# The last weight chunks of a block product rounded and split in another order, the fourth in a tile of its own, and a half-bank copy moved

## The chip, the cores and the metric

The kernel runs on one core of one Trainium2 chip. The time is device microseconds of one launch; lower is better. TensorE is called PE here, VectorE DVE, ScalarE ACT, GpSimd POOL; SP issues transfers.

## The reference

One decoder block on a sequence of 512 positions with model width 1024, in float32: a gated sub-layer with two mixers, then RMSNorm with modulation, a SwiGLU feed-forward of width 2816 with a gated residual, and a final RMSNorm. What matters here is the end:

```python
f_g, f_u = jnp.split(h2 @ w_ffn_in, 2, axis=-1)
x = x + gate2 * ((jax.nn.silu(f_g) * f_u) @ w_ffn_out)
...
return rms_norm(x, final_norm_g)
```

## The kernel before

**Precision.** Every float32 operand of a matmul is kept as a rounded half "hi" and a remainder "lo", and one product is three matmuls (`mm3`, L53 to L55: hi x hi, hi x lo, lo x hi). For a weight chunk (256 rows x 512 columns, 512 KB) ACT makes hi (the *rounding*, L114, "ACTIVATE hi<-raw") and DVE makes lo = raw - hi (the *split*, L118).

**Weights** come as a stream. `add_w` appends a chunk to it, with `where` as the home of its two halves; without one they rotate through three pairs of tiles named hi and lo. `issue` loads a raw chunk through SP's queue into one of three raw tiles, so the load of a chunk waits for the split of the chunk three before it. `get(i, ahead)` sees to it that the stream is rounded and split up to `ahead` chunks past i. Within an engine everything runs in the order of the program text (`manual_schedule`); waits between engines are put in by the framework from the tiles that are read and written.

**The end.** The down projection (gate product times w_ffn_out) is computed as seven block products after a Strassen-like scheme. Each accumulator Z[n] is two PSUM banks, one for each tile of 128 positions; Z[0] and Z[1] belong to positions 0 to 255 (tiles 0, 1), Z[2] and Z[3] to 256 to 511 (tiles 2, 3); even n holds columns 0 to 511, odd n columns 512 to 1023. `zprod` runs a block product chunk by chunk, with a list of tasks for the other engines at each chunk; `plain` adds the two rows of weight tiles that the scheme leaves over (its chunks are W_FO, here called the W_FO chunks). The last block product, key (1, 1), has five chunks (`zs`, called chunk 0 to 4, or the first to the fifth) and adds into Z[1] alone. It is written out as three passes: e = 0 (tile 0, 512 columns wide), then e = 1 in two passes of 256 columns. The second of these writes another bank, `last`, into which ACT copies the right half of Z[1][1] beforehand (the *half-bank copy*, L1867 before).

**Residuals.** `res(n, tk)` is a multiply by the gate (DVE, L1258), an add into x (DVE, L1259) and a square with a sum (ACT, L1263). `row_rstd` sums a row's parts (DVE, L1269, the *row sum*) and raises to -1/2 on POOL (L1270); `finish` scales the row (DVE, L1781) and stores it; `scale_g` (L1769) multiplies by the norm's gain ahead of `finish_last`.

**Order before the change.** Chunk 0 is rounded with the last `get` in `zprod`, chunk 1 after residual (0, 1), chunk 2 right behind it; chunk 3 after residual (3, 2), when the loop begins; chunk 4 in the loop, after the residuals (3, 3), (2, 2) and (2, 3). Homes: chunk 0 S2 tiles 6 and 7, chunk 1 S2 tiles 2 and 3, chunk 2 E1, chunks 3 and 4 the rotating pairs.

Of the kernel before, what the change touches and what calls it, by code (L numbers as in the profile page):

```python
# [10 lines left out]
F32R = mybir.dt.float32r  # L11
I32 = mybir.dt.int32
AF = mybir.ActivationFunctionType
# [15 lines left out]
def block_kernel(ctx: ExitStack, tc: tile.TileContext, x, positions, w_ada, b_ada, w_in,  # L29
# [3 lines left out]
    T, V, A, P, SY = nc.tensor, nc.vector, nc.scalar, nc.gpsimd, nc.sync  # L33
    ctx.enter_context(tc.manual_schedule())
    base = ctx.enter_context(tc.tile_pool(name="base", bufs=1))
# [6 lines left out]
    def bank(k, name="bank"):  # L42
        return psum.tile([128, 512], F32, name=name, tag=f"b{k}", bufs=1)

    def f(ap):
        return ap.bitcast(F32)
# [4 lines left out]
    def mm3(o, wl, rl, start, stop, **kw):  # L51
        (wh, wlo), (rh, rlo) = wl, rl
        T.matmul(o, wh, rh, start=start, stop=False, **kw)  # L53
        T.matmul(o, wh, rlo, start=False, stop=False, **kw)  # L54
        T.matmul(o, wlo, rh, start=False, stop=stop, **kw)  # L55


    stream, wseq, chunk = [], [], {}
# [5 lines left out]
    def add_w(src, kts, c0, n, lo=None, where=None):  # L64
        stream.append(dict(kind="w", src=src, kts=kts, c0=c0, n=n, lo=lo or V, where=where))
        wseq.append(len(stream) - 1)
        return len(stream) - 1
# [29 lines left out]
    def prep(i):  # L97
        e = stream[i]
        if e["kind"] == "m":
            e["fn"](e["raw"])  # L100
            return
        m = len(e["kts"]) * e["n"]
        if e["where"] is None:
            hi = base.tile([128, 1024], F32R, name="hi", tag="hi", bufs=3)
            lo = base.tile([128, 1024], F32R, name="lo", tag="lo", bufs=3)
        elif isinstance(e["where"], tuple):
            hi, lo = (s2home(k, name="wx") for k in e["where"])
        else:
            t = ffn[0].tile([128, 2, 1024], F32R, name="wx", tag=e["where"], bufs=1)
            hi, lo = t[:, 0], t[:, 1]  # L110
        if i == W1[0]:
            V.tensor_copy(hi[:, :m], e["raw"][:, :m])
        else:
            A.activation(hi[:, :m], e["raw"][:, :m], AF.Copy)  # L114
        if e["lo"] == "later":
            e["do"] = lambda: V.tensor_sub(lo[:, :m], e["raw"][:, :m], f(hi[:, :m]))
        else:
            e["lo"].tensor_sub(lo[:, :m], e["raw"][:, :m], f(hi[:, :m]))  # L118
        chunk[i] = (e["view"](hi), e["view"](lo))

    def ensure(upto):
        upto = min(upto, len(stream) - 1, st["limit"] - 1)
        while True:
            for i in range(st["prep"], min(st["prep"] + 16, len(stream), st["limit"])):
                if "raw" in stream[i]:
                    continue
                if room(i):
                    issue(i)
                elif stream[i]["kind"] == "w" or not stream[i]["mid"]:
                    break  # L130
            if st["prep"] > upto:
                break
            prep(st["prep"])
            st["prep"] += 1
# [13 lines left out]
    def get(i, ahead=2):  # L148
        k = wseq.index(i)
        ensure(wseq[min(k + ahead, len(wseq) - 1)])  # L150
        return chunk[i]
# [37 lines left out]
    ffn = []  # L189
# [113 lines left out]
    W_Z = {}  # L303

    def add_z(key, where=(None,) * 5):
        W_Z[key] = []
        for c in range(5):
            if key in wsum:
                src, k0, c0 = wsum[key], 2 * c, 0
            else:  # L310
                src, k0, c0 = w_ffn_out, KZ[key[0]][2 * c], key[1] * 512
            W_Z[key].append(add_w(src, [k0, k0 + 1], c0, 512, where=where[c]))
# [3 lines left out]
    W_FO = [add_w(w_ffn_out, KC, 0, 512, where="E7")]  # L316
    add_z(4)
    W_FO.append(add_w(w_ffn_out, KC, 512, 512, where="E0"))
    add_z((1, 1), ((6, 7), (2, 3), "E1", None, None))

    def wsum_steps():

# [26 lines left out]
    for i in range(4):  # L349
        t = base.tile([128, D], F32, name=f"x{i}", tag=f"X{i}", bufs=1)  # L350
# [31 lines left out]
    ch = chain.append  # L382
# [175 lines left out]
    for kt in range(8):  # L558
        hi, lo = chunk[W1[kt]]
# [338 lines left out]
    for h in range(2):  # L898
        pb = [bank(b, "pav") for b in range(4)]
        for i in W_AV[h]:  # L900
# [10 lines left out]
            hi, lo = get(i)  # L911
# [353 lines left out]
    def resid(p, c0, n, slot, tk, gate):  # L1265
        resid_b(resid_a(p, c0, n, tk, gate), c0, n, slot, tk)

    def row_rstd(tk):
        V.tensor_reduce(r2[:, tk:tk + 1], ss2[:, tk], op=OP.add, axis=AX.X)  # L1269
        P.tensor_tensor(r2[:, tk:tk + 1], r2[:, tk:tk + 1], mhalf[:, :1], op=OP.pow)  # L1270
# [179 lines left out]
    for half in range(2):  # L1450
        for h in range(2):
            po = O[2 * half + h]

            def res(e):
                resid(po[e], 512 * h, 512, h, 2 * half + e, gate_b[1])

            for n_, i in enumerate(W_O[2 * h:2 * h + 2]):
                hi, lo = chunk[i]
# [177 lines left out]
    for half in range(2):  # L1636
        o = slice(half * 256, (half + 1) * 256)
        for w in range(2):
            for ci, i in enumerate(W_F[w]):
                hi, lo = chunk[i]  # L1640
# [126 lines left out]
    def scale_g(c0, n, tk):  # L1767
        cs_ = slice(c0, c0 + n)
        V.tensor_mul(x_out()[tk][:, cs_], xt[tk][:, cs_], fng[0][:, cs_])  # L1769
# [10 lines left out]
    def finish(tk):  # L1780
        V.scalar_tensor_tensor(x_out()[tk], xt[tk], r2[:, tk:tk + 1], fng[0], op0=OP.mult, op1=OP.mult)  # L1781
        SY.dma_start(out[tk * 128:(tk + 1) * 128, :], xo[tk])


    Z, ZB = {}, ((4, 7), (0, 1), (2, 3), (5, 6))

    def zprod(k, ka, kw, start, tasks):
        if start:
            Z[k] = [bank(ZB[k][e], "pfo") for e in range(2)]
        for c, i in enumerate(W_Z[kw]):  # L1790
            wh, wl = get(i)
            for fn in tasks[c]:
                fn()
            ah, al = za[ka, c // 2]
            for e in range(2):
                o = slice(e * 128, (e + 1) * 128)
                for j in range(2):
                    k_ = 2 * (c % 2) + j
                    mm3(Z[k][e], (ah[:, k_, o], al[:, k_, o]), (wh[:, j], wl[:, j]),
                        start and c + j == 0, c + j == 5, skip_group_check=True)  # L1800
# [12 lines left out]
    def z_add(dst, src, op):  # L1813
        for e in range(2):
            op(Z[dst][e], Z[dst][e], Z["s", src][e])

    def hi_(key, c):
        return lambda: a_hi(key, c)

    def lo_(key, c):  # L1820
        return lambda: a_lo(key, c)
# [30 lines left out]
    def plain(o, tk, n, c=slice(0, 512)):  # L1852
        hi, lo = get(W_FO[n])
        opt_a_mm(o, tk, hi[:, :, c], lo[:, :, c], KC, gT, 22, False)
# [4 lines left out]
    def res(n, tk):  # L1859
        return lambda: resid(Z[n][tk % 2], 512 * (n % 2), 512, n % 2, tk, gate_b[2])  # L1860

    zprod(2, "A22", 4, False, [[hi_("S4", 2), lo_("S4", 2)], [lambda: z_add(3, 2, V.tensor_sub)],
                               [lambda: z_add(1, 3, V.tensor_add)], [res(0, 0)], [res(0, 1)]])
    zs = W_Z[1, 1]
    ch = [get(zs[0])]
    last = bank(7, "pfo")
    A.activation(last[:, :256], Z[1][1][:, 256:], AF.Copy)  # L1867
    for tk in range(2):
        plain(Z[3][tk], 2 + tk, 1)
    scale_g(0, 512, 1)  # L1870
    ch.append(get(zs[1], 1))
    res(3, 2)()
    for tk in range(2):
        plain(Z[2][tk], 2 + tk, 0)
    ch.append(get(zs[2], 1))
    tasks = {(0, 0): [res(3, 3)], (0, 1): [res(2, 2), lambda: row_rstd(2)], (0, 2): [res(2, 3), lambda: row_rstd(3)],
             (0, 3): [lambda: finish(2)], (0, 4): [lambda: finish(3)]}
    for e, z in ((0, None), (1, 0), (1, 1)):
        c = slice(0, 512) if z is None else slice(256 * z, 256 * z + 256)
        o = Z[1][0] if z is None else (Z[1][1], last)[z][:, :256]  # L1880
        t = slice(e * 128, (e + 1) * 128)
        n = c.stop - c.start
        for k, i in enumerate(zs):
            if k == len(ch):
                ch.append(get(i, 1))
            hi, lo = ch[k]
            for fn in tasks.pop((e, k), []):
                fn()
            ah, al = za["S4", k // 2]
            for j in range(2):  # L1890
                k_ = 2 * (k % 2) + j
                mm3(o, (ah[:, k_, t], al[:, k_, t]), (hi[:, j, c], lo[:, j, c]), False, False, skip_group_check=True)
        plain(o, e, 1, c)
        if z is None:
            resid(o, 512, n, 1, e, gate_b[2])
            row_rstd(e)
            finish(e)
        elif z == 0:
            resid(o, 512, n, 1, e, gate_b[2])
            scale_g(512, n, e)  # L1900
        else:
            resid(o, 768, n, 2, e, gate_b[2])
            row_rstd(e)
            scale_g(768, n, e)
            finish_last(e)
# [49 lines left out]
```

## Time and profile before

| | us |
|---|---|
| median of 3 runs | 813.89 (813.73 to 814.85) |
| the profiled execution's own time | 813.89 |
| span of the profile, first to last instruction | 812.1 |
| PE busy | 792.3 (98%) |
| weight load busy | 705.6 (87%) |
| DVE busy | 689.2 (85%) |
| ACT busy | 422.8 (52%) |
| chain that ended last, share of PE | 89% |

The profile shows one execution. Times in it count from the first instruction; a row of the timeline gives start and duration in us, engine, line, operation, output and inputs, and in brackets how long the engine sat idle before it and what released it. A busy PE is matmuls in a pipeline, whose ends are modelled, so that rows overlap: the spacing of starts tells the rate. The stretch that the change touches runs from about 765 us to the end.

### The profile page before, as it was taken

The numbers are of one execution on the slowest core, as the hardware profiler recorded it, in microseconds if no ns is written. First come the engines' busy times: TensorE is split into PE (matmuls) and PEld (weight loads), VectorE is DVE, ScalarE is ACT, GpSimd is POOL, SyncE is SP. The second block draws the span as 40 slices with busy tenths as digits, with TensorE's granted clock in tenths as the row PEclk, the third lists the DMA queues.
The fourth block names the chain that finished last, engine by engine and source line by source line (L and its number), as shares of the span: only waits on it lengthen the run. The fifth ranks groups of instructions, "written<-read, shape, count | busy, mean of one in ns | idle before, by whom it ended". The sixth has DMA issues, their size and how long they took to land.

```text
span 812.1 us, 12511 instructions
## 1 busy us (share of the span) xinstructions
PE 792.3 (98%) x4746; PEld 705.6 (87%) x4746; DVE 689.2 (85%) x1153; ACT 422.8 (52%) x727; POOL 137.2 (17%) x141
## 2 busy tenths in 40 slices
PE   7999999999999999999999999999999999999966
PEld 7889888888888888898888899999999999888855
DVE  7989788898899877787698779898999998987764
ACT  6674445323322255665536586566655556756441
POOL 3060031362344411000000011201111110000000
PEclk9999999999999999999999999999999999999998
DMA  9964352434336741147630528989997975556522
GB/s 317 336 174 120 104 182 79 115 92 130 110 123 207 222 142 52 52 157 233 196 117 25 183 78 200 265 230 253 273 274 199 281 193 173 178 185 199 191 77 105
DMA packets 104844, 138.44 MB, mean 170 GB/s; under 512 B 6560, under 2 KB 72736, under 8 KB 104624
## 3 DMA queue, kind: packets, MB, share of 16 engines
q1 hardware_dynamic: 92608, 106.15, 41.5%
q0 software_dynamic: 9584, 27.07, 14.2%
q10 hardware_dynamic: 2592, 4.42, 1.5%
q8 instruction: 37, 0.61, 0.3%
q14 instruction: 23, 0.19, 0.1%
HBM read 135.26 MB, written 23.07 MB: 195 GB/s over the span
## 4 chain that ended last, share of the span: by engine, by line
PE 89%; DVE 5%; ACT 3%; issue 2%; DMA 1%; POOL 0%; POOLq 0%; SPq 0%; ACTq 0%; DVEq 0%
PE pb L55 9%; PE pb L54 9%; PE pb L53 9%; PE R L54 8%; PE R L55 8%; PE R L53 8%; PE pfo L54 3%; PE pfo L55 3%; PE pfo L53 3%; PE pgb L53 2%; PE pgb L54 2%; PE pgb L55 2%; PE pav L54 2%; PE pav L53 2%; PE pav L55 2%
## 5 line engine op out<-in xcount | busy, mean ns | idle before, releaser
L114 ACT ACTIVATE hi<-raw 128x1024 fp32r<-128x1024 f32 (+2 forms) x98 | 101.5, 1039 | 87.3 <-DMA raw<-in_w_proj_a_dram 22.8
L54 PE MATMUL pb<-s,hi 128*128 128x512 f32 (+1 forms) x320 | 122.8, 384 | 0.0
L53 PE MATMUL pb<-s,hi 128*128 128x512 f32 (+1 forms) x256 | 98.8, 386 | 0.0
L55 PE MATMUL pb<-s,lo 128*128 128x512 f32 (+1 forms) x256 | 97.9, 383 | 0.0
L118 DVE TENSOR_TENSOR lo<-raw,hi 128x1024 fp32r<-128x1024 f32 (+2 forms) x62 | 75.1, 1214 | 26.0 <-ACT hi L114 25.7
L118 POOL TENSOR_TENSOR lo<-raw,hi 128x1024 fp32r<-128x1024 f32 x29 | 73.0, 2518 | 131.2 <-ACT hi L114 130.2
L54 PEld LDWEIGHTS pb<-s,hi 128*128 128x128 f32 x320 | 60.1, 188 | 10.9
L55 PEld LDWEIGHTS pb<-s,lo 128*128 128x128 f32 x256 | 48.1, 188 | 8.8
L53 PEld LDWEIGHTS pb<-s,hi 128*128 128x128 f32 x256 | 48.1, 188 | 8.4
L205 DVE SCALAR_TENSOR_TENSOR acc<-mraw,cols,acc 128x512 f32<-128x512 f32 x49 | 43.1, 879 | 3.7 <-DMA mraw<-in_w_ada_dram 2.9
L1270 POOL TENSOR_TENSOR sm<-sm,mhalf 128x1 f32<-128x1 f32 x8 | 5.3, 660 | 231.1 <-DVE sm L1269 231.1
L55 PE MATMUL R<-tb,sx 128*128 128x256 f32 x160 | 44.2, 276 | 0.0
L53 PE MATMUL R<-tb,hi 128*128 128x256 f32 x160 | 44.2, 276 | 0.0
L54 PE MATMUL R<-tb,hi 128*128 128x256 f32 x160 | 44.2, 276 | 0.0
L55 PE MATMUL R<-tb,lo 128*128 128x256 f32 x160 | 44.2, 276 | 0.0
L53 PE MATMUL R<-tb,sx 128*128 128x256 f32 x160 | 44.2, 276 | 0.0
L54 PE MATMUL R<-tb,sx 128*128 128x256 f32 x160 | 44.2, 276 | 0.0
L334 POOL DMA_DIRECT2D wsum<-in_w_ffn_out_dram x20 | 17.8, 892 | 95.2 <-DMA wsum<-wsum 57.6
L53 PE MATMUL pfo<-hi,s 128*128 128x512 f32 (+1 forms) x68 | 26.4, 388 | 5.6 <-ACT hi L114 5.6
L55 PEld LDWEIGHTS R<-tb,sx 128*128 128x128 f32 x160 | 30.0, 188 | 0.0
L53 PEld LDWEIGHTS R<-tb,hi 128*128 128x128 f32 x160 | 30.0, 188 | 0.0
L54 PEld LDWEIGHTS R<-tb,hi 128*128 128x128 f32 x160 | 30.0, 188 | 0.0
(429 smaller groups left out, 2534.5 us busy)
## 6 DMA issues: line engine op xcount, KB each, us to landing
raw<-in_w_ffn_in_dram SPq DMA_DIRECT2D x44, 512.0 KB, 6.9
raw<-in_w_in_dram SPq DMA_DIRECT2D x40, 512.0 KB, 3.8
wsum<-in_w_ffn_out_dram POOLq DMA_DIRECT2D x30, 512.0 KB, 7.7
mraw<-in_w_ada_dram SPq DMA_DIRECT2D x20, 512.0 KB, 3.8
raw<-wsum SPq DMA_DIRECT2D x20, 512.0 KB, 4.0
raw<-in_w_ffn_out_dram SPq DMA_DIRECT2D x18, 512.0 KB, 4.3
eraw<-in_w_ada_dram SPq DMA_DIRECT2D x30, 256.0 KB, 4.8
wsum<-wsum POOLq DMA_DIRECT2D x10, 512.0 KB, 6.1
```

What stands on the lines that cost most here:

```text
L53: T.matmul(o, wh, rh, start=start, stop=False, **kw)
L54: T.matmul(o, wh, rlo, start=False, stop=False, **kw)
L55: T.matmul(o, wlo, rh, start=False, stop=stop, **kw)
L114: A.activation(hi[:, :m], e["raw"][:, :m], AF.Copy)
L118: e["lo"].tensor_sub(lo[:, :m], e["raw"][:, :m], f(hi[:, :m]))
L205: V.scalar_tensor_tensor(o, w, cs[:, j:j + 1], o, op0=OP.mult, op1=OP.add)
L334: P.dma_start(wsum[n][o], src, accum_op=OP.add)
L1270: P.tensor_tensor(r2[:, tk:tk + 1], r2[:, tk:tk + 1], mhalf[:, :1], op=OP.pow)
```

## The change

Chunks are rounded and split at other places of the program (`ahead(i)` is `get` without looking further): chunk 0 ahead of residual (0, 0), chunk 1 ahead of (0, 1), chunk 2 ahead of (3, 2), chunks 3 and 4 ahead of (3, 3). Chunk 3 gets tile S1_0 as its home, whose place in the base pool held a part of the gate product before. The half-bank copy and the `scale_g` of tile 1 go behind the residuals of tiles 2 and 3. The tasks within the e = 0 pass stand behind the matmuls of their chunk in the text.

```diff
--- before.py
+++ after.py
@@ -106,7 +106,8 @@
         elif isinstance(e["where"], tuple):
             hi, lo = (s2home(k, name="wx") for k in e["where"])
         else:
-            t = ffn[0].tile([128, 2, 1024], F32R, name="wx", tag=e["where"], bufs=1)
+            pool = base if e["where"].startswith("S1") else ffn[0]
+            t = pool.tile([128, 2, 1024], F32R, name="wx", tag=e["where"], bufs=1)
             hi, lo = t[:, 0], t[:, 1]
         if i == W1[0]:
             V.tensor_copy(hi[:, :m], e["raw"][:, :m])
@@ -316,7 +317,7 @@
     W_FO = [add_w(w_ffn_out, KC, 0, 512, where="E7")]
     add_z(4)
     W_FO.append(add_w(w_ffn_out, KC, 512, 512, where="E0"))
-    add_z((1, 1), ((6, 7), (2, 3), "E1", None, None))
+    add_z((1, 1), ((6, 7), (2, 3), "E1", "S1_0", None))
 
     def wsum_steps():
 
@@ -1859,37 +1860,40 @@
     def res(n, tk):
         return lambda: resid(Z[n][tk % 2], 512 * (n % 2), 512, n % 2, tk, gate_b[2])
 
+    zs = W_Z[1, 1]
+
+    def ahead(i):
+        return lambda: get(i, 0)
+
     zprod(2, "A22", 4, False, [[hi_("S4", 2), lo_("S4", 2)], [lambda: z_add(3, 2, V.tensor_sub)],
-                               [lambda: z_add(1, 3, V.tensor_add)], [res(0, 0)], [res(0, 1)]])
-    zs = W_Z[1, 1]
-    ch = [get(zs[0])]
-    last = bank(7, "pfo")
-    A.activation(last[:, :256], Z[1][1][:, 256:], AF.Copy)
+                               [lambda: z_add(1, 3, V.tensor_add)], [ahead(zs[0]), res(0, 0)], [ahead(zs[1]), res(0, 1)]])
     for tk in range(2):
         plain(Z[3][tk], 2 + tk, 1)
-    scale_g(0, 512, 1)
-    ch.append(get(zs[1], 1))
+    ahead(zs[2])()
     res(3, 2)()
     for tk in range(2):
         plain(Z[2][tk], 2 + tk, 0)
-    ch.append(get(zs[2], 1))
-    tasks = {(0, 0): [res(3, 3)], (0, 1): [res(2, 2), lambda: row_rstd(2)], (0, 2): [res(2, 3), lambda: row_rstd(3)],
-             (0, 3): [lambda: finish(2)], (0, 4): [lambda: finish(3)]}
+    ahead(zs[3])()
+    ahead(zs[4])()
+    res(3, 3)()
+    last = bank(7, "pfo")
+    tasks = {1: [res(2, 2), lambda: row_rstd(2)], 2: [res(2, 3), lambda: row_rstd(3)],
+             3: [lambda: A.activation(last[:, :256], Z[1][1][:, 256:], AF.Copy), lambda: finish(2)],
+             4: [lambda: finish(3), lambda: scale_g(0, 512, 1)]}
     for e, z in ((0, None), (1, 0), (1, 1)):
         c = slice(0, 512) if z is None else slice(256 * z, 256 * z + 256)
         o = Z[1][0] if z is None else (Z[1][1], last)[z][:, :256]
         t = slice(e * 128, (e + 1) * 128)
         n = c.stop - c.start
         for k, i in enumerate(zs):
-            if k == len(ch):
-                ch.append(get(i, 1))
-            hi, lo = ch[k]
-            for fn in tasks.pop((e, k), []):
-                fn()
+            hi, lo = chunk[i]
             ah, al = za["S4", k // 2]
             for j in range(2):
                 k_ = 2 * (k % 2) + j
                 mm3(o, (ah[:, k_, t], al[:, k_, t]), (hi[:, j, c], lo[:, j, c]), False, False, skip_group_check=True)
+            if z is None:
+                for fn in tasks.pop(k, []):
+                    fn()
         plain(o, e, 1, c)
         if z is None:
             resid(o, 512, n, 1, e, gate_b[2])
```

ACT at the end of the kernel, from the rounding of the second W_FO chunk (wx_7886) on. Before; raw_7850, 7870, 7889, 7909 and 7931 are chunks 0 to 4, and xr0 to xr3 the rows of the residual that are squared:

```order
L114 ACTIVATE wx_7886<-raw_7830 128x1024
L1263 ACTIVATE rt_7891,ss2_71<-xr0_3776 128x512
L114 ACTIVATE s2_77<-raw_7850 128x1024
L1263 ACTIVATE rt_7911,ss2_71<-xr1_3778 128x512
L114 ACTIVATE wx_7927<-raw_7870 128x1024
L114 ACTIVATE wx_7933<-raw_7889 128x1024
L1867 ACTIVATE pfo_7936<-pfo_7389 128x256
L1263 ACTIVATE rt_7953,ss2_71<-xr2_3780 128x512
L114 ACTIVATE hi_7969<-raw_7909 128x1024
L1263 ACTIVATE rt_7973,ss2_71<-xr3_3782 128x512
L1263 ACTIVATE rt_7983,ss2_71<-xr2_3780 128x512
L1263 ACTIVATE rt_7995,ss2_71<-xr3_3782 128x512
```

In the changed kernel, from the row after that rounding on, where raw_7893 and raw_7915 are chunks 3 and 4:

```order
L115 ACTIVATE s2_77<-raw_7850 128x1024
L1264 ACTIVATE rt_7895,ss2_71<-xr0_3776 128x512
L115 ACTIVATE wx_7911<-raw_7870 128x1024
L1264 ACTIVATE rt_7917,ss2_71<-xr1_3778 128x512
L115 ACTIVATE wx_7945<-raw_7889 128x1024
L1264 ACTIVATE rt_7948,ss2_71<-xr2_3780 128x512
L115 ACTIVATE wx_7964<-raw_7893 128x1024
L115 ACTIVATE hi_7967<-raw_7915 128x1024
L1264 ACTIVATE rt_7971,ss2_71<-xr3_3782 128x512
L1264 ACTIVATE rt_7988,ss2_71<-xr2_3780 128x512
L1264 ACTIVATE rt_8000,ss2_71<-xr3_3782 128x512
L1881 ACTIVATE pfo_7975<-pfo_7389 128x256
```

The roundings of chunks 3 and 4 follow one another ahead of the squares of xr3, xr2 and xr3, and the half-bank copy, which stood ahead of the first square of xr2, closes the row.

DVE, from the first residual of tile 2 (pfo_7392) on. Before:

```order
L1258 TENSOR_TENSOR rt_7953<-pfo_7392,gate2b_4486 128x512
L1259 TENSOR_TENSOR xr2_3780<-xr2_3780,rt_7953 128x512
L118 TENSOR_TENSOR lo_7970<-raw_7909,hi_7969 128x1024
L1258 TENSOR_TENSOR rt_7973<-pfo_7393,gate2b_4486 128x512
L1259 TENSOR_TENSOR xr3_3782<-xr3_3782,rt_7973 128x512
L1258 TENSOR_TENSOR rt_7983<-pfo_7599,gate2b_4486 128x512
L1259 TENSOR_TENSOR xr2_3780<-xr2_3780,rt_7983 128x512
L1269 TENSOR_REDUCE sm_66<-ss2_71 128x1
L1258 TENSOR_TENSOR rt_7995<-pfo_7600,gate2b_4486 128x512
L1259 TENSOR_TENSOR xr3_3782<-xr3_3782,rt_7995 128x512
L1269 TENSOR_REDUCE sm_66<-ss2_71 128x1
L118 TENSOR_TENSOR lo_8008<-raw_7931,hi_8007 128x1024
```

In the changed kernel:

```order
L1259 TENSOR_TENSOR rt_7948<-pfo_7392,gate2b_4486 128x512
L1260 TENSOR_TENSOR xr2_3780<-xr2_3780,rt_7948 128x512
L119 TENSOR_TENSOR wx_7964<-raw_7893,wx_7964 128x1024
L119 TENSOR_TENSOR lo_7968<-raw_7915,hi_7967 128x1024
L1259 TENSOR_TENSOR rt_7971<-pfo_7393,gate2b_4486 128x512
L1260 TENSOR_TENSOR xr3_3782<-xr3_3782,rt_7971 128x512
L1259 TENSOR_TENSOR rt_7988<-pfo_7599,gate2b_4486 128x512
L1260 TENSOR_TENSOR xr2_3780<-xr2_3780,rt_7988 128x512
L1270 TENSOR_REDUCE sm_66<-ss2_71 128x1
L1259 TENSOR_TENSOR rt_8000<-pfo_7600,gate2b_4486 128x512
L1260 TENSOR_TENSOR xr3_3782<-xr3_3782,rt_8000 128x512
L1270 TENSOR_REDUCE sm_66<-ss2_71 128x1
```

Both splits stand ahead of the residual of pfo_7393. Before, the last split closed the row, behind two row sums (TENSOR_REDUCE). The `scale_g` of xr1, which stood just ahead of these rows, now follows two `finish` that come behind them.

PE at the seam of e = 0 and e = 1, with the engine that a matmul waits for in brackets. Before (pfo_7388 is Z[1][0], pfo_7389 Z[1][1]):

```order
L54 MATMUL pfo_7388<-wx_7886,gs_7692 128x512
L55 MATMUL pfo_7388<-wx_7886,gs_7692 128x512
L53 MATMUL pfo_7389<-s2_77,za_7751 128x256
L54 MATMUL pfo_7389<-s2_77,za_7751 128x256
L55 MATMUL pfo_7389<-s2_77,za_7751 128x256
```

In the changed kernel:

```order
L54 MATMUL pfo_7388<-wx_7886,gs_7692 128x512
L55 MATMUL pfo_7388<-wx_7886,gs_7692 128x512
L53 MATMUL pfo_7389<-s2_77,za_7751 128x256 [waits Activation_49]
L54 MATMUL pfo_7389<-s2_77,za_7751 128x256
L55 MATMUL pfo_7389<-s2_77,za_7751 128x256
```

The order of the matmuls is the same; the first one of 256 columns has got a wait for ACT, whose copy reads the other half of pfo_7389.

## The prediction

> **What bounds the kernel now.** I read the waits of TensorE (PE) over the last 95 us first: engine, line, what it waited for, us in total, times, longest.
>
> ```profile
> span 812.1 us, 12511 instructions
> PE pfo L53 <- ACT hi L114: 5.6, 2, 5.3
> PE pfo L54 <- DVE lo L118: 1.2, 2, 0.8
> ```
>
> Up to 783 us PE streams without a hole, so what the change may win lies behind it. The timeline from there (start, duration, engine, line, in brackets the idle time before it) shows both holes:
>
> ```profile
> 778.95 0.40 PE L53 MATMUL pfo<-s,za 128*128 128x512 f32 x1
> 780.34 0.39 PE L53 MATMUL pfo<-wx,za 128*128 128x512 f32 x1
> 783.56 0.50 PE L53 MATMUL pfo<-hi,s 128*128 128x512 f32 x1 [0.30 <-ACT hi L114]
> 784.82 0.50 PE L54 MATMUL pfo<-lo,s 128*128 128x512 f32 x1 [0.76 <-DVE lo L118]
> 785.85 0.40 PE L55 MATMUL pfo<-hi,s 128*128 128x512 f32 x1
> ...
> 788.27 0.16 DVE L1269 TENSOR_REDUCE sm<-ss 128x1 f32<-128x5 f32 x1 [0.85 <-ACT rt L1263]
> 788.34 0.68 DVE L1258 TENSOR_TENSOR rt<-pfo,gate2b 128x512 f32<-128x512 f32 x1
> 789.84 0.63 ACT L1263 ACTIVATE rt<-xr 128x512 f32<-128x512 f32 x1 [1.61 <-DVE xr L1259]
> 791.55 1.23 DVE L118 TENSOR_TENSOR lo<-raw,hi 128x1024 fp32r<-128x1024 f32 x1 [0.72 <-ACT hi L114]
> 791.57 0.79 PE L53 MATMUL pfo<-hi,s 128*128 128x512 f32 x1 [5.32 <-ACT hi L114]
> 792.69 2.47 DVE L1781 SCALAR_TENSOR_TENSOR xo<-xr,sm,fng 128x1024 f32<-128x1024 f32 x2
> 796.74 0.28 PE L53 MATMUL pfo<-s,za 128*128 128x256 f32 x1
> 796.94 0.69 DVE L1258 TENSOR_TENSOR rt<-pfo,gate2b 128x512 f32<-128x512 f32 x1 [1.78 <-PE pfo L55]
> 805.34 0.42 DVE L1258 TENSOR_TENSOR rt<-pfo,gate2b 128x256 f32<-128x256 f32 x1 [2.77 <-PE pfo L55]
> ```
>
> The first hole (0.30 + 0.76) is the fourth chunk of block product (1,1), whose rounding sits on ACT behind the square of one residual. The second (5.32) is the fifth, which sits behind the squares of three more; its rounded half appears only after the last of them (789.84), its split at 791.55. The e = 0 pass ends late for that, the two 256-column passes of e = 1 run from 796.74, and their last residual starts at 805.34, as soon as PE's last matmul lets it. From 805.34 to the end of the span (6.76) nothing is changed. So the question is when that multiply (the "end multiply" below) starts.
>
> Third view, busy time in stretches of 0.4 us: stretch, length, PE, weight load, DVE, ACT, POOL, then the granted clock.
>
> ```profile
> 788.40:788.80 0.40, 0.00 (x0) 0.00 (x0) 0.40 (x2) 0.00 (x0) 0.29 (x1) 1.00 0.00 0
> 788.80:789.20 0.40, 0.00 (x0) 0.00 (x0) 0.37 (x2) 0.00 (x0) 0.28 (x1) 0.51 0.00 0
> 795.20:795.60 0.40, 0.40 (x3) 0.30 (x2) 0.00 (x0) 0.00 (x0) 0.00 (x0) 0.50 0.89 369
> 795.60:796.00 0.40, 0.40 (x3) 0.36 (x2) 0.00 (x0) 0.00 (x0) 0.00 (x0) 0.96 1.07 440
> 809.20:809.60 0.40, 0.00 (x0) 0.00 (x0) 0.00 (x0) 0.00 (x0) 0.00 (x0) 0.60 0.97 390
> ```
>
> The clock halves at 788.8, 2.6 us after the last matmul before the hole ended (785.85 + 0.40), and comes back at 795.6, after some 3 us of matmuls at half rate. It halves again at 809.3. The distances, 6.8 and 13.7 us, are as 1 to 2: the decision seems to fall on a grid of about 3.4 us (estimate), and PE was busy for about a quarter of the stretch 785.4 to 788.8 that ended in a drop.
>
> **The change, step by step.** No instruction is added or taken away; 512 KB loads, roundings and splits are the same. They change places on ACT and DVE, and the loads are released earlier. The durations that the replay needs:
>
> ```profile
> 765.09 0.37 SPq L94 DMA_DIRECT2D raw<-in_w_ffn_out_dram  x1
> DMA to landing us min/median/max: 3.7/4.0/4.7
> 766.47 1.05 ACT L114 ACTIVATE wx<-raw 128x1024 fp32r<-128x1024 f32 x1
> 768.94 1.21 DVE L118 TENSOR_TENSOR wx<-raw,wx 128x1024 fp32r<-128x1024 f32 x1
> 770.07 0.68 DVE L1258 TENSOR_TENSOR rt<-pfo,gate2b 128x512 f32<-128x512 f32 x1
> 770.79 0.69 DVE L1259 TENSOR_TENSOR xr<-xr,rt 128x512 f32<-128x512 f32 x1
> 771.51 0.63 ACT L1263 ACTIVATE rt<-xr 128x512 f32<-128x512 f32 x1 [4.00 <-DVE xr L1259]
> 772.14 1.04 ACT L114 ACTIVATE s<-raw 128x1024 fp32r<-128x1024 f32 x1
> 773.22 1.23 DVE L118 TENSOR_TENSOR s<-raw,s 128x1024 fp32r<-128x1024 f32 x1 [1.74 <-ACT s L114]
> 776.43 1.99 ACT L114 ACTIVATE wx<-raw 128x1024 fp32r<-128x1024 f32 x2
> 778.33 0.36 ACT L1867 ACTIVATE pfo<-pfo 128x256 f32<-128x256 f32 x1
> 779.79 0.69 DVE L1769 TENSOR_TENSOR xo<-xr,fng 128x512 f32<-128x512 f32 x1
> 780.39 0.68 DVE L1258 TENSOR_TENSOR rt<-pfo,gate2b 128x512 f32<-128x512 f32 x1
> 798.45 0.63 ACT L1263 ACTIVATE rt<-xr 128x512 f32<-128x512 f32 x1 [6.94 <-DVE xr L1259]
> 799.21 0.16 DVE L1269 TENSOR_REDUCE sm<-ss 128x1 f32<-128x5 f32 x1 [0.85 <-ACT rt L1263]
> 800.03 1.28 DVE L1781 SCALAR_TENSOR_TENSOR xo<-xr,sm,fng 128x1024 f32<-128x1024 f32 x1 [0.66 <-POOL sm L1270]
> 801.23 0.42 DVE L1258 TENSOR_TENSOR rt<-pfo,gate2b 128x256 f32<-128x256 f32 x1
> 802.14 0.42 DVE L1769 TENSOR_TENSOR xo<-xr,fng 128x256 f32<-128x256 f32 x1
> ```
>
> As starts after starts: rounding to split 1.08 (772.14, 773.22); split to the next on DVE 1.13 (768.94, 770.07); multiply to add 0.72 (770.07, 770.79); multiply to square 1.44 to 1.51 (770.07 to 771.51, 796.94 to 798.45); square to next ACT work 0.63 (772.14); two roundings in a row 0.95 apart (776.43, two in 1.99); square to row sum 0.76 (798.45, 799.21), and 0.07 on to the next DVE work (788.27, 788.34).
>
> *Chunk 0.* Its load is issued at 765.09 as before and lands about 768.9. ACT is free since 767.4, so it rounds at 768.9 to 769.0, and DVE splits at 770.1, right behind the W_FO split. Residual (0,0) slides from 770.07 to 771.2.
> *Chunks 1 and 2.* Square of (0,0) at 772.7, rounding 773.3, split 774.4, residual (0,1) 775.5, square 776.9, rounding 777.6, split 778.7, residual (3,2) 779.8. ACT and DVE wait for one another in turn; no time is won yet, the splits are done at 775.6 and 779.9, and PE wants them at 780.34 and 781.7.
> *Chunks 3 and 4.* Square 781.2, roundings 781.9 and 782.8, splits 782.95 and 784.1, done 784.2 and 785.3. The loads are no limit: released by the splits of chunks 0 and 1 (771.3 and 775.6), even at the longest landing (4.7) there by 776.0 and 780.3. PE reaches chunk 3 at 783.1 with the rounded half ready; its second matmul, due at 783.3, waits for the split until 784.2, 0.6 earlier than the 784.82 of today. Chunk 4 follows without a hole. So the hole of 5.32 is gone, and e = 0 ends at 784.2 + 17 x 0.23 = 788.2 (five matmuls of chunk 3, six of chunk 4, six of W_FO; 0.23 is a sixth of 778.95 to 780.34).
> *The fourth chunk's home* costs no instruction; the last reader of what lay in its place, a split of a part of A22, stands far ahead on DVE, in the product before, so the rounding waits for its load alone.
> *Residuals (3,3), (2,2), (2,3).* Multiplies at 785.2, 786.6 (two operations of 0.68 later) and 788.9 (0.07 behind a row sum), squares at 786.7, 788.1 and 790.4, row sums at 788.8 and 791.2.
> *The half-bank copy* (0.36) is now on ACT behind the last of these squares: 790.4 + 0.63 = 791.0, done 791.4. Ahead of the first 256-column matmul stands a wait on ACT that the order before did not have: the copy reads the other half of the bank that these matmuls write. Queued behind it on PE are all 72 narrow matmuls, and for those the last two residuals wait. PE is idle from 788.2 to 791.45, 3.2 us. Moved copy and new wait have no row in the trace; bounds: if the wait were free, PE would go on at 788.2, and if one more square came ahead of the copy (0.76), at 792.2. I take 791.45.
> The Trainium skill, "PSUM — Partial Sum Buffer", section "PSUM bank collisions raise a hardware error", says that two engines must be kept off one bank even at different columns. By it the wait is real; without it the end multiply would fall to DVE at 799.9 (below), 808.5. No run here shows a collision.
> *End of PE at full clock.* 791.45 + (805.34 - 796.74) = 800.05 for the end multiply.
> *End of DVE.* finish(2) at 791.3, finish(3) at 792.5 (two in 2.47), scale_g 793.7, residual (1,0) 794.3 (0.60 after it, as 779.79 to 780.39), its row sum 796.6 (796.94 to 799.21), finish(0) 797.4, first narrow residual 798.6, scale_g 799.5 (801.23 to 802.14), end multiply possible at 799.9. scale_g, 0.6 us on DVE, now stands in this chain; before, it stood at 779.79, ahead of a wait. DVE and PE arrive within 0.15 us: hardly any slack is left on either side.
> *The clock.* 3.2 us of idle PE is longer than the 2.6 after which it halved above. On a grid of 3.4 us whose place against the program I can't know, the idle time covers 1.6 to 3.2 of one stretch. If a quarter busy is the most that still drops, 44% of the places drop; if half busy drops too, 94%. A drop lasts one stretch, less what of it is still idle, at half rate: 1.0 to 1.7 us, mostly 1.6. I take the drop, as what the trace is nearest to: end multiply at 801.65.
>
> The sum: 805.34 - 801.65 = 3.7 us earlier. The profiled execution's own time is 813.89 (span 812.1 and 1.8 around it), which is also the median of the three runs: 813.9 - 3.7 = 810.2.
>
> **Rivals.** *B, the clock holds.* The idle 3.2 us fall on two stretches, each busy enough. For it: the grid is free and the idle time is shorter than one step. Against: 2.6 us were enough once. Then 805.34 - 800.05 = 5.3 earlier: 808.6.
> The Trainium skill, "TensorE: Matmul & The Clock Gate", section "HAM oscillation — how this bites in real kernels", allows idle gaps up to about 3.4 us. By that rule B is what happens, 808.6. The trace speaks against a limit so sharp, with its drop 2.6 us after the last matmul.
> *C, the hand-overs cost more.* From 770 to 791 ACT and DVE hand over to each other some ten times; 0.1 more at each delays the copy and both ends by 1.0, 811.2; a second stretch at half clock instead costs 1.7 more, 811.9. For it: the trains of hand-overs are serial, with no slack between 772.7 and 791.4. Against: every step of them has its row in the trace.
> *D, the change doesn't do what it says:* chunk 4 still waits, behind a load or a square. Its load has 2.5 us to spare and the order puts both splits ahead of residual (3,3), so only something unseen could do it: within 0.2% of 813.9.
> *E, slower.* The half clock stays: the narrow matmuls behind the copy don't count as busy enough, and all 8.6 us of them take 17.2. End multiply at 808.65, 3.3 later than today: 817.2. Against it: after 791.57 three us of matmuls at half rate brought the clock back. It gets slower than before by more than 0.2% only where 2 x (5.3 + 1.6) = 13.8 us pass at half clock, four steps of the grid.
>
> **Numbers.** Likeliest, one step at half clock: 0.52, 810.2. B 0.30, C 0.09, D 0.05, E 0.04. The first two alone span 808.6 to 810.3. The free wait (808.5) with half of the 1.1 us by which the three runs before differ sets the low end, 808.0; the later copy (0.75) and the same half set the high one at 811.8 with C's first kind in it. D, E and part of C are left out. 0.2% is 1.6 us, about what tells a change from none here; A, B and C are all faster by more: 0.91 faster, 0.05 same, 0.04 slower.
>
> **What would show it.** In the profile after: no wait of PE for the rounding of a chunk longer than 1 us in the last 35 us; the chunk-3 split within 0.5 of 782.95; a new PE wait on ACT's copy of about 3.2 us before the first 256-column matmul; DVE's end multiply nearly back to back with finish(0)'s followers; clock rows with 0.50 for about 3.4 us from about 789 to 795, or none (B). Wrong would be: a hole still at the fifth chunk, no wait at the copy, or a last multiply that starts after 803.

## The result and the profile after

| | median, us | range, us | runs |
|---|---|---|---|
| before | 814.12 | 813.73 to 814.85 | 5 |
| changed | 809.28 | 807.76 to 810.6 | 5 |

The changed kernel takes 0.994 of the time before (95% interval 0.9925 to 0.9956), 4.8 us less. The forecast was 810.2, with a range from 808.0 to 811.8. The profiled execution was the slowest of its five: 810.6, with a span of 808.8.

The waits of PE over the last 95 us of the profile after:

```profile
PE pfo L53 <- ACT pfo L1881: 3.0, 1, 3.0
PE pfo L54 <- DVE wx L119: 0.7, 1, 0.7
```

The hole of 5.3 us at the fifth chunk is gone, and so is PE's wait for ACT's rounding of the fourth. In its place stands one wait of 3.0 for the half-bank copy (L1881), which is the new wait that the prediction named. Lines of the code after the first insertion are one higher than before (L1258 is now L1259, L1781 is L1782).

The timeline of the same execution (start, duration, engine, line, in brackets the idle time before it and what ended it):

```profile
778.03 0.40 PE L53 MATMUL pfo<-s,za 128*128 128x512 f32 x1
782.02 1.23 DVE L119 TENSOR_TENSOR wx<-raw,wx 128x1024 fp32r<-128x1024 f32 x1 [1.74 <-ACT wx L115]
783.30 0.50 PE L54 MATMUL pfo<-wx,s 128*128 128x512 f32 x1 [0.72 <-DVE wx L119]
787.07 0.39 PE L55 MATMUL pfo<-wx,gs 128*128 128x512 f32 x1
789.45 0.63 ACT L1264 ACTIVATE rt<-xr 128x512 f32<-128x512 f32 x1 [1.61 <-DVE xr L1260]
790.08 0.36 ACT L1881 ACTIVATE pfo<-pfo 128x256 f32<-128x256 f32 x1
790.38 1.28 DVE L1782 SCALAR_TENSOR_TENSOR xo<-xr,sm,fng 128x1024 f32<-128x1024 f32 x1
790.50 0.58 PE L53 MATMUL pfo<-s,za 128*128 128x256 f32 x1 [3.04 <-ACT pfo L1881]
790.51 1.56 POOL L1271 TENSOR_TENSOR sm<-sm,mhalf 128x1 f32<-128x1 f32 x1 [1.82 <-DVE sm L1270]
792.11 1.29 DVE L1782 SCALAR_TENSOR_TENSOR xo<-xr,sm,fng 128x1024 f32<-128x1024 f32 x1 [0.44 <-POOL sm L1271]
797.00 1.28 DVE L1782 SCALAR_TENSOR_TENSOR xo<-xr,sm,fng 128x1024 f32<-128x1024 f32 x1 [0.67 <-POOL sm L1271]
799.11 0.42 DVE L1770 TENSOR_TENSOR xo<-xr,fng 128x256 f32<-128x256 f32 x1
802.07 0.42 DVE L1259 TENSOR_TENSOR rt<-pfo,gate2b 128x256 f32<-128x256 f32 x1 [2.53 <-PE pfo L55]
```

Everything ahead of the change ran 0.92 us earlier in this execution than in the one of before (the first e = 0 matmul at 778.03, there 778.95). Nothing that the change touches stands there, and the same start lies between 777.49 and 778.66 in six of the eight runs below, at 780.00 and 781.07 in the other two. So I measure from that matmul to the end multiply, and call it the stretch: before 805.34 - 778.95 = 26.39, after 802.07 - 778.03 = 24.04, forecast 801.65 - 778.95 = 22.70.

The clock, in three steps of 3.41 us around the drop, then in two ahead of the next drop (columns: from and to, length, busy time of PE, PE's weight load, DVE, ACT and POOL, granted clock, and two of DMA):

```profile
786.46:789.87 3.41, 1.00 (x5) 0.49 (x3) 2.02 (x4) 1.20 (x4) 0.56 (x1) 1.00 0.00 0
789.87:793.28 3.41, 2.78 (x13) 2.78 (x14) 2.56 (x3) 0.57 (x3) 1.56 (x1) 0.50 0.24 96
793.28:796.70 3.42, 3.42 (x18) 3.42 (x18) 2.17 (x5) 0.72 (x2) 0.29 (x1) 0.50 0.52 213
800.11:803.52 3.41, 1.92 (x17) 1.72 (x15) 0.85 (x2) 0.48 (x2) 0.00 (x0) 1.00 0.08 31
803.52:806.94 3.42, 0.00 (x0) 0.00 (x0) 1.04 (x3) 0.65 (x2) 0.66 (x1) 1.00 0.30 119
```

The clock drops at 789.87 and is half until 796.70, so two steps of the grid and not the one that the prediction charged. That is why the stretch is 1.34 longer than forecast.

### The profile page after: what moved, and what is told of

Read it like the earlier page. It is cut to its first block, busy times and chain, and to the rows that moved or that the text cites. A ratio compares the mean times of both kernels' runs of the same rounds, so it can differ in the third digit from the quotient of the medians.

```text
span 808.8 us, 12510 instructions
## 1 busy us (share of the span) xinstructions
PE 791.9 (98%) x4746; PEld 706.2 (87%) x4746; DVE 688.5 (85%) x1153; ACT 423.0 (52%) x727; POOL 139.2 (17%) x141
## 4 chain that ended last, share of the span: by engine, by line
PE 61%; DVE 14%; ACT 2%; issue 2%; POOL 0%; POOLq 0%; ACTq 0%; DVEq 0%
PE R L54 8%; PE R L55 8%; PE R L53 8%; PE pb L53 3%; PE pb L55 3%; PE pb L54 3%; PE pfo L54 3%; PE pfo L55 3%; PE pfo L53 3%; DVE sco L735 2%; DVE m L731 2%; PE pgb L53 2%; PE pgb L54 2%; PE pgb L55 2%; PE po L53 2%; PE po L54 2%
## 5 line engine op out<-in xcount | busy, mean ns | idle before, releaser
L1271 POOL TENSOR_TENSOR sm<-sm,mhalf 128x1 f32<-128x1 f32 x8 | 6.3, 788 | 226.3 <-DVE sm L1270 226.3
L206 DVE SCALAR_TENSOR_TENSOR acc<-mraw,cols,acc 128x512 f32<-128x512 f32 x49 | 40.4, 824 | 3.1 <-DMA mraw<-in_w_ada_dram 2.4
L53 PEld LDWEIGHTS R<-tb,hi 128*128 128x128 f32 x160 | 30.0, 188 | 0.0
L54 PEld LDWEIGHTS R<-tb,sx 128*128 128x128 f32 x160 | 30.0, 188 | 0.0
L55 PEld LDWEIGHTS R<-tb,sx 128*128 128x128 f32 x160 | 30.0, 188 | 0.0
L55 PEld LDWEIGHTS R<-tb,lo 128*128 128x128 f32 x160 | 30.0, 188 | 0.0
```

The lines of the kernel that those rows point to most:

```text
L206: V.scalar_tensor_tensor(o, w, cs[:, j:j + 1], o, op0=OP.mult, op1=OP.add)
```

## The experiments

Eight runs follow, in two groups of four; each group ran on one chip, beside the kernel before. The first row of the table repeats the result above, which was timed by itself.

| run | median, us | ratio to before, 95% interval | stretch in its profile, us |
|---|---|---|---|
| changed kernel | 809.28 | 0.9940 (0.9925 to 0.9956) | 24.04 |
| copy early | 808.69 | 0.9946 (0.9927 to 0.9965) | 21.43 |
| nine products in the hole | 808.51 | 0.9932 (0.9920 to 0.9944) | 21.42 |
| rotating home | 811.53 | 0.9981 (0.9962 to 1.0000) | 22.48 |
| fifth chunk late | 813.38 | 0.9996 (0.9982 to 1.0010) | 26.86 |
| squares behind | 803.14 | 0.9856 (0.9820 to 0.9891) | 16.88 |
| gain first | 808.13 | 0.9919 (0.9894 to 0.9943) | 20.86 |
| changed kernel again | 810.74 | 0.9954 (0.9932 to 0.9976) | 22.72 |
| rotating home again | 810.33 | 0.9944 (0.9922 to 0.9967) | 22.73 |

The kernel before had a median of 814.16 beside the first group and 814.36 beside the second.

### Undoing one part: the copy early

The half-bank copy goes back to where nothing waits for it, ahead of residual (3,2); all else stays.

```diff
     ahead(zs[2])()
+    last = bank(7, "pfo")
+    A.activation(last[:, :256], Z[1][1][:, 256:], AF.Copy)
     res(3, 2)()
...
     res(3, 3)()
-    last = bank(7, "pfo")
...
-             3: [lambda: A.activation(last[:, :256], Z[1][1][:, 256:], AF.Copy), lambda: finish(2)],
+             3: [lambda: finish(2)],
```

> The changed kernel with one thing undone: the half-bank copy stands ahead of residual (3,2) again, on ACT in a wait. Theory (the copy's new place makes PE wait 3.0 us at the seam, and the clock drop that follows makes the spread 807.8 to 810.6): no wait of PE at the seam, no half clock there, the end multiply bound by DVE at about 799.3, so 807.6 to 808.6 with runs within 0.6 of each other. Rival (the wait is covered by DVE's chain anyway, so the copy's place is worth nothing): 809.3 as the changed kernel, with its spread.

Measured: 808.69 (807.55 to 813.47). PE has no wait at the seam, and its clock first drops at 800.94, behind its last matmul, as expected, but the time is just above the expected 808.6, and the runs spread over 5.9 us and not 0.6, so the late copy is not the only cause of a spread. The timeline of this run: the start of e = 0, the two finishes with POOL's power between them, PE's last matmul and the end multiply.

```profile
778.66 0.40 PE L53 MATMUL pfo<-s,za 128*128 128x512 f32 x1
791.02 1.29 DVE L1782 SCALAR_TENSOR_TENSOR xo<-xr,sm,fng 128x1024 f32<-128x1024 f32 x1
791.15 1.56 POOL L1271 TENSOR_TENSOR sm<-sm,mhalf 128x1 f32<-128x1 f32 x1 [1.83 <-DVE sm L1270]
792.75 1.29 DVE L1782 SCALAR_TENSOR_TENSOR xo<-xr,sm,fng 128x1024 f32<-128x1024 f32 x1 [0.44 <-POOL sm L1271]
796.26 0.28 PE L55 MATMUL pfo<-wx,gs 128*128 128x256 f32 x1
800.09 0.42 DVE L1259 TENSOR_TENSOR rt<-pfo,gate2b 128x256 f32<-128x256 f32 x1
```

PE's last matmul now starts 3.8 us ahead of the end multiply: PE is early, and the end waits for DVE's chain. Against the two-step execution of the changed kernel this is 24.04 - 21.43 = 2.61 off the stretch, against a one-step one (22.72, below) 1.29. The medians, 808.69 and 809.28, lie closer than that, and their intervals overlap: that an early copy helps is shown in the profiles, its size in the time is not.

### Taking away the half clock alone: nine products in the hole

Nine 128x128 float32 products whose result nobody reads go into bank 4 between the e = 0 and the first e = 1 pass. They keep PE busy for 2.17 us (787.14 to 789.31) of the time for which it waits.

```diff
         if z is None:
             resid(o, 512, n, 1, e, gate_b[2])
+            wb = bank(4, "warm2")
+            for _ in range(9):
+                T.matmul(wb[:, :128], ident, ident, start=True, stop=True)
```

> The changed kernel with nine matmuls of 128 columns into an unused bank between the e = 0 and the e = 1 pass, about 2.8 us of PE work in a hole of 3.0; the copy stays late. They compute nothing that is used. Theory (the clock, not the wait itself, costs what lies between 807.8 and 810.6): granted clock 1.00 through the seam, all runs at 807.6 to 808.8. Rival (the wait alone sets the time, the clock hardly counts because DVE is nearly as late): unchanged, 809.3 with the spread of the changed kernel.

Measured: 808.51 (807.81 to 808.96, the upper end 0.16 above what was expected). Its timeline:

```profile
777.87 0.40 PE L53 MATMUL pfo<-s,za 128*128 128x512 f32 x1
790.34 0.39 PE L53 MATMUL pfo<-s,za 128*128 128x256 f32 x1 [1.03 <-ACT pfo L1881]
798.74 0.28 PE L55 MATMUL pfo<-wx,gs 128*128 128x256 f32 x1
799.29 0.42 DVE L1259 TENSOR_TENSOR rt<-pfo,gate2b 128x256 f32<-128x256 f32 x1
```

Its busy time and clock in two steps from the end of e = 0 on:

```profile
786.90:790.30 3.40, 2.41 (x20) 2.17 (x18) 1.63 (x5) 1.72 (x5) 0.56 (x1) 1.00 0.00 0
790.30:793.70 3.40, 3.36 (x28) 3.36 (x29) 2.96 (x3) 0.00 (x0) 1.56 (x1) 1.00 0.38 157
```

The first narrow matmul stands at 12.47 us behind the start of e = 0 (790.34 - 777.87), where it also stands in the changed kernel (790.50 - 778.03). So the wait on the copy is untouched, and still the clock stays at 1.00 and the stretch is 21.42, the same as with the early copy. The wait alone is hidden behind DVE's chain, whose end multiply starts 0.55 after PE's last matmul does and waits for nothing; only the half clock on top of it makes PE the later side. The medians, 808.51 and 809.28, can't show this, since their intervals overlap.

### Undoing one part: the fourth chunk in the rotating pair

```diff
-    add_z((1, 1), ((6, 7), (2, 3), "E1", "S1_0", None))
+    add_z((1, 1), ((6, 7), (2, 3), "E1", None, None))
```

> The changed kernel, but chunk 3 goes into the rotating pair again instead of tile S1_0. Theory (the home costs and brings nothing, its rotating pair is free long before 781.9): same as the changed kernel, 807.8 to 810.6. Rival (the home is what lets chunk 3 and 4 be rounded in a row, since the rotating pair is still read by block product 4): rounding of chunk 4 waits for PE, a hole of 1 us or more before chunk 4, 811 or later.

Measured: 811.53 over five runs from 808.53 to 815.33, but its profiled execution, the fastest of them, has the waits of the changed kernel and nothing else. Time and profile disagreed, so it ran again, beside the changed kernel as it is, on one chip.

> The changed kernel unchanged, to stand on the same chip beside the run with the rotating home. 808 to 810.6, middle 809.3, as in its first timing.

> The changed kernel with the fourth chunk back in the rotating pair of buffers, once more, since its first three rounds (811.53) and its profile (the same waits as the changed kernel's) disagree. Theory (the home is worth nothing, because the pair's buffer is free before the fourth chunk's split): within 0.8 us of the changed kernel beside it. Rival (the home is worth something that the profiled execution does not show): 1.5 to 2.5 us later than the changed kernel beside it.

Measured: 810.33 with the rotating home, 810.74 with a home of its own, 12 runs each. With the rotating home, PE's waits and then the two ends of the stretch in the timeline:

```profile
PE pfo L53 <- ACT pfo L1881: 3.0, 1, 3.0
PE pfo L54 <- DVE lo L119: 0.7, 1, 0.7
```

```profile
778.10 0.40 PE L53 MATMUL pfo<-s,za 128*128 128x512 f32 x1
800.83 0.42 DVE L1259 TENSOR_TENSOR rt<-pfo,gate2b 128x256 f32<-128x256 f32 x1 [1.21 <-PE pfo L55]
```

The changed kernel as it is beside it, the same two ends, and its clock around the hole:

```profile
777.65 0.40 PE L53 MATMUL pfo<-s,za 128*128 128x512 f32 x1
800.37 0.42 DVE L1259 TENSOR_TENSOR rt<-pfo,gate2b 128x256 f32<-128x256 f32 x1 [1.20 <-PE pfo L55]
```

```profile
786.67:790.08 3.41, 0.43 (x2) 0.01 (x1) 1.62 (x5) 1.72 (x5) 0.56 (x1) 1.00 0.00 0
790.08:793.49 3.41, 3.36 (x15) 3.36 (x16) 2.97 (x3) 0.00 (x0) 1.56 (x1) 0.50 0.38 156
```

The home of its own is worth nothing: 22.73 against 22.72 in the stretch. The 2 us by which it was later in the first group did not come back and have no counterpart in its profile. The second execution of the changed kernel shows more: here the clock was half for one step (790.08 to 793.49), as forecast, and the stretch came out at 22.72 where 22.70 was forecast.

### Undoing one part: the fifth chunk late

Only the rounding and split of the fifth chunk go back behind residual (2,3).

```diff
     ahead(zs[3])()
-    ahead(zs[4])()
     res(3, 3)()
...
-    tasks = {1: [res(2, 2), lambda: row_rstd(2)], 2: [res(2, 3), lambda: row_rstd(3)],
+    tasks = {1: [res(2, 2), lambda: row_rstd(2)], 2: [res(2, 3), lambda: row_rstd(3), ahead(zs[4])],
```

> The changed kernel, but chunk 4 is rounded and split behind residual (2,3), as before the change; chunks 0 to 3 stay ahead, the copy late. Theory (the gain comes from chunk 4 leaving the place behind the three residuals): the hole at the fifth chunk is back with 4 to 5 us, the drop of the clock in it, time 813 to 815, as before. Rival (the gain comes from chunks 0 to 3 being earlier): 809 to 811.

Measured: 813.38, ratio 0.9996: the whole gain is gone. Waits of PE:

```profile
PE pfo L53 <- ACT hi L115: 5.3, 1, 5.3
PE pfo L54 <- DVE wx L119: 0.7, 1, 0.7
PE pfo L54 <- DVE lo L119: 0.5, 1, 0.5
```

Its clock in four steps from the end of the chunks ahead of the hole on:

```profile
785.72:789.13 3.41, 1.42 (x5) 0.86 (x5) 3.15 (x5) 0.82 (x3) 0.00 (x0) 1.00 0.00 0
789.13:792.54 3.41, 0.00 (x0) 0.00 (x0) 1.60 (x4) 1.80 (x5) 0.68 (x2) 0.50 0.00 0
792.54:795.95 3.41, 2.40 (x5) 1.61 (x6) 2.89 (x3) 0.76 (x2) 0.43 (x1) 0.50 0.02 7
795.95:799.36 3.41, 3.41 (x10) 2.63 (x9) 1.33 (x2) 0.00 (x0) 0.00 (x0) 0.50 0.76 308
```

The hole of 5.3 is back, with a drop of the clock that lasts three steps in this execution. The fifth chunk's place is what the change is worth; the other moves, which this run keeps, bring nothing without it.

### What else stands in the chain: gain first, and squares behind

With the early copy DVE sets the end, and it stands still for 0.44 us between finish(2) and finish(3) (791.02 + 1.29 to 792.75), waiting for a power on POOL that takes 1.56 there and 0.55 elsewhere. So scale_g was put between the power and finish(2), with the copy early (the edit is against the run with the early copy):

```diff
-             3: [lambda: finish(2)],
-             4: [lambda: finish(3), lambda: scale_g(0, 512, 1)]}
+             3: [lambda: scale_g(0, 512, 1), lambda: finish(2)],
+             4: [lambda: finish(3)]}
```

> The run with the early copy, with scale_g put ahead of finish(2). There the power on GpSimd for row 3 took 1.56 us beside finish(2), against 0.55 us elsewhere, and VectorE stood 0.44 us waiting for it. Theory (only the finish slows the power): the power falls beside scale_g and takes 0.55 to 0.7 us, VectorE does not wait, 0.4 us less than the early copy alone: 808.2. Rival (any VectorE instruction of that length slows it, or VectorE is not the one that sets the end): power 1.2 us or more, or no gain; 808.7 as the early copy alone.

Measured: 808.13 (806.98 to 814.06). DVE and POOL in its timeline:

```profile
778.42 0.40 PE L53 MATMUL pfo<-s,za 128*128 128x512 f32 x1
790.75 0.68 DVE L1770 TENSOR_TENSOR xo<-xr,fng 128x512 f32<-128x512 f32 x1
790.91 0.93 POOL L1271 TENSOR_TENSOR sm<-sm,mhalf 128x1 f32<-128x1 f32 x1 [1.83 <-DVE sm L1270]
791.35 2.47 DVE L1782 SCALAR_TENSOR_TENSOR xo<-xr,sm,fng 128x1024 f32<-128x1024 f32 x2
799.28 0.42 DVE L1259 TENSOR_TENSOR rt<-pfo,gate2b 128x256 f32<-128x256 f32 x1
```

The two finishes are back to back again (two in 2.47), and the stretch is 20.86, 0.57 less than with the early copy alone. The power is still slowed, to 0.93, so the statement that only the finish slows it falls; it only no longer makes DVE wait. The medians can't tell 808.13 from 808.69.

The last run takes every cause found out of the way at once: each square on ACT stands behind the next chunk's rounding, the copy behind the rounding of the fourth chunk, scale_g between the row sums, and both finishes ahead of the loop. resid is used in its two halves, resid_a (DVE) and resid_b (the square on ACT with its sum), through helpers res_a and res_b. The helpers and the removal of the tasks from the loop are left out here:

```diff
...
-                               [lambda: z_add(1, 3, V.tensor_add)], [ahead(zs[0]), res(0, 0)], [ahead(zs[1]), res(0, 1)]])
+                               [lambda: z_add(1, 3, V.tensor_add)], [ahead(zs[0]), res_a(0, 0)],
+                               [ahead(zs[1]), res_b(0, 0), res_a(0, 1)]])
+    ahead(zs[2])()
+    res_b(0, 1)()
     for tk in range(2):
         plain(Z[3][tk], 2 + tk, 1)
-    ahead(zs[2])()
-    res(3, 2)()
+    res_a(3, 2)()
+    ahead(zs[3])()
+    last = bank(7, "pfo")
+    A.activation(last[:, :256], Z[1][1][:, 256:], AF.Copy)
+    res_b(3, 2)()
+    res_a(3, 3)()
     for tk in range(2):
         plain(Z[2][tk], 2 + tk, 0)
-    ahead(zs[3])()
     ahead(zs[4])()
-    res(3, 3)()
...
+    res_b(3, 3)()
+    res_a(2, 2)()
+    res_b(2, 2)()
+    res_a(2, 3)()
+    row_rstd(2)
+    res_b(2, 3)()
+    scale_g(0, 512, 1)
+    row_rstd(3)
+    finish(2)
+    finish(3)
...
```

> Every square of the last residuals stands behind the next chunk's rounding on ScalarE instead of ahead of it, the half-bank copy stands behind the rounding of the fourth chunk, scale_g stands between the row sums, and finish(2) and finish(3) stand ahead of the loop. Theory (what is left of the hole at the fourth chunk, 0.7 us, and the copy's wait, 3.0 us, both come from where a ScalarE instruction is queued; TensorE at a full clock needs no more): no wait of TensorE over 0.5 us between the first product of the last block and its last one, no rows at half clock there, and the end multiply is released by TensorE about 7 us earlier than in the changed kernel's profile (802.07): near 795 to 797, a time of 803 to 805.5. Rival (the bank that the narrow products go to, or VectorE's own chain of residuals, row sums and finishes, is next): the end multiply comes no earlier than in the run with nine extra products (799.29), a time of 807.5 to 809.

Measured: 803.14 (802.89 to 805.4), 0.9856 of the time before, and 7.6 us under the changed kernel on the same chip.

```profile
780.00 0.40 PE L53 MATMUL pfo<-s,za 128*128 128x512 f32 x1
796.57 0.28 PE L55 MATMUL pfo<-wx,gs 128*128 128x256 f32 x1
796.88 0.42 DVE L1259 TENSOR_TENSOR rt<-pfo,gate2b 128x256 f32<-128x256 f32 x1 [1.99 <-PE pfo L55]
```

The profiled execution is the slowest of the six (805.4), with its start of e = 0 at 780.00; the stretch is 16.88. Its waits list none of PE after 720 us, and the end multiply starts as soon as PE's last matmul lets it. The stretch is now PE's work alone: 36 matmuls of 0.23 for e = 0 and 8.60 for the narrow ones make 16.9. So the theory holds: what lay beyond PE's own work there came from the order in which the instructions of ACT and DVE are queued. Which of the moves gives how much, this run doesn't tell apart. This version beats both kernels.

## Why the prediction was right, step by step

*The fifth chunk's hole.* Right. It is gone, and undoing this alone gives the whole gain back (813.38).

*The replay of ACT and DVE up to the copy.* Right to a few hundredths, counted from the first e = 0 matmul, forecast and then the profile after: the chunk-3 split 4.00 and 3.99, PE going on behind it 5.25 and 5.27, the first narrow matmul 12.50 and 12.47, finish(2) 12.35 and 12.35. The hand-overs cost what their rows before said; rival C's first half (0.1 more at each) did not happen.

*The new wait on the copy.* Right: 3.2 forecast, 3.04 measured, the difference because the row of PE's last e = 0 matmul ends later (9.43 after the start of e = 0, forecast 9.25). The half-bank copy in its new place costs PE this wait and, through it, the clock.

*The fourth chunk's home.* Costed at nothing, and worth nothing (22.73 and 22.72).

*The clock.* Right in kind, its size open. Of four profiled executions with this wait (the changed kernel twice, the rotating home twice) all four dropped, three for one step, with stretches of 22.48, 22.72 and 22.73, and one for two, with 24.04. Rival B, in which the clock holds, was seen in none of them. The mean granted clock of the executions that were only timed says that it does happen. In 31 of the 34 executions with this wait it is 0.995 or 0.996, in one 0.997, and in two, of 807.76 and 810.26 us, 0.998, as with the nine products (0.998 to 0.999). 0.998 leaves about 3.2 us at half clock in all (0.002 of 806 us, twice); one step at the hole (3.41) and the drop behind PE's last matmul, at least 1.6 to the end of the span in this case's profiles, would take 5 (estimate). So in these two the clock held at the hole. The Trainium skill, "TensorE: Matmul & The Clock Gate", section "HAM oscillation — how this bites in real kernels", allows idle gaps up to about 3.4 us; here a gap of 3.0 was enough four times, so the measurement decides against it as a bound on one gap. What a drop costs is half of PE's busy time at the half clock, as forecast: on top of the 21.07 of a full clock (12.47 + 8.60) that gives 21.07 + 3.36/2 = 22.75 for the second execution of the changed kernel (22.72), 21.07 + 2.84/2 = 22.49 for the rotating home (22.48) and 21.07 + (2.78 + 3.42)/2 = 24.17 for the first execution (24.04), so it holds to 0.13. The second step was rival C's other half, at its price of 1.7; how often it comes, the prediction had no row for.

*DVE's chain.* Mis-sized by 0.53. I took two finishes in 2.47, as before. But there both powers were done before the first finish began, at 792.69, as POOL's row in the timeline of before shows:

```profile
790.91 0.55 POOL L1270 TENSOR_TENSOR sm<-sm,mhalf 128x1 f32<-128x1 f32 x1 [1.83 <-DVE sm L1269]
```

After the change row_rstd(3) stands directly ahead of finish(2), so its power falls beside the finish, takes 1.56 and holds back finish(3): 13.55 forecast, 14.08 measured, and from there on everything on DVE is as much later (finish(0) 18.45 and 18.97, the second scale_g 20.55 and 21.08). It is hidden where the clock drops, since PE ends later still; where the clock holds, DVE sets the end (21.42 with the nine products, where 21.10 was forecast from PE). That the time, 808.51, is what rival B forecast, 808.6, is in part luck: B ended with PE, and the stretch is 0.32 longer than its 21.10.

*The sum.* 810.2 forecast, 809.28 and 810.74 measured. The changed kernel against the kernel beside it gained 4.8 and 3.6; the forecast gain was 3.7. The earlier stages move by about a microsecond from one execution to the next, so agreement of the medians to less than that is luck. The stretch leaves those stages out; its agreement to 0.02 (22.72 for 22.70) is in part luck too, since the three one-step executions spread over 0.25, but that all three lie within 0.22 of the forecast is not.

## What to carry to other kernels

When an engine's queue holds both work that the critical engine waits for and work that only a late sum needs, put the first ahead of the second one instruction at a time: here the change gave 3.6 to 4.8 us, all of it lost again with the fifth chunk's rounding and split put back, and the remaining squares, the copy, scale_g and the finishes together gave 7.6 more. A moved instruction that shares a bank or a buffer with the critical engine carries its wait with it, so look at what it now stands behind. And price an idle gap on PE by its length and by half of what PE does afterwards at half clock.

## What the runs showed of the hardware

*The clock is decided step by step on a grid of 3.41 us, by how busy PE was in the step that ends.* In ten steps whose rows are quoted here the busy time and the decision at the end can be read, first at full and then at half clock, by rising share. The rows not shown yet, in the same columns, are one of the first run with the rotating home and two of the run with the fifth chunk late, behind its last matmuls:

```profile
789.39:792.80 3.41, 2.84 (x13) 2.84 (x14) 2.62 (x4) 0.52 (x3) 1.56 (x1) 0.50 0.25 101
806.20:809.61 3.41, 1.69 (x15) 1.49 (x13) 1.01 (x4) 0.51 (x2) 0.00 (x0) 1.00 0.00 0
809.61:813.03 3.42, 0.00 (x0) 0.00 (x0) 0.88 (x2) 0.61 (x1) 0.66 (x1) 1.00 0.37 145
```

| run | step | PE busy in it | clock after it |
|---|---|---|---|
| changed again | 786.67 to 790.08 | 0.43 (13%) | drops |
| changed | 786.46 to 789.87 | 1.00 (29%) | drops |
| fifth chunk late | 785.72 to 789.13 | 1.42 (42%) | drops |
| fifth chunk late | 806.20 to 809.61 | 1.69 (50%) | stays full |
| changed | 800.11 to 803.52 | 1.92 (56%) | stays full |
| nine products | 786.90 to 790.30 | 2.41 (71%) | stays full |
| fifth chunk late | 792.54 to 795.95 | 2.40 (70%) | stays half |
| changed | 789.87 to 793.28 | 2.78 (81%) | stays half |
| rotating home | 789.39 to 792.80 | 2.84 (83%) | rises |
| changed again | 790.08 to 793.49 | 3.36 (99%) | rises |

So a full clock was lost at 42% and less and kept at 50% and more, and a half clock came back at 83% and more but not at 81% and less; the shares are approximate, since the ends of matmuls are modelled. This explains one step against two: in the execution with 24.04 the drop came 0.63 us before PE went on (789.87, 790.50), and that was enough idle time in the first step to keep the clock down for a second. The Trainium skill, "TensorE: Matmul & The Clock Gate", section "What's actually happening", gives a free-running window of 3413 ns; the distances here agree (789.87 to 796.70 is two of 3.41). The length of a gap alone does not decide: by these bounds (estimates from the rows) 3.04 idle us keep the clock in 12 to 28% of their places on the grid, those where neither step gets more than 1.72 to 1.99 of them (3.41 less the 1.69 and the 1.42 of the table), and cost two steps in 12 to 22%. By the mean clock above it was kept in two or three of 34, nearer the low end. The steps of the other runs agree with the table; no run set the busy share by design, so where between 42 and 50%, and between 81 and 83%, the bounds lie stays open.

*A power on POOL beside DVE.* The same 128x1 instruction (L1271) took 0.55 to 0.57 with DVE idle or reading one operand from PSUM, 0.93 beside scale_g and 1.56 beside a finish. Both times it began just behind the DVE instruction and ended 0.41 after it (790.51 + 1.56 against 790.38 + 1.28 in the profile after, 790.91 + 0.93 against 790.75 + 0.68 with the gain first), as though it had waited for the whole of it. The Trainium skill, "SBUF — State Buffer", section "Who interferes with whom", says that a DVE instruction with two inputs in SBUF contends with a POOL instruction that reads SBUF, over a pair of ports that works as an exclusive lock. The rows agree: finish and scale_g read both tensors from SBUF, and the power, which came second, took 0.38 and 1.01 longer than its 0.55. With the rule in hand the prediction would have seen finish(3) half a microsecond later.
